# Column sums for a norm: folding 128 partitions to 64, so that one matmul with the ones replaces two

## The chip, the cores and the metric

The kernel runs on one core of a Trainium2 chip. The metric is the device time of one execution in microseconds (us); the median of three runs is taken. TensorE (PE in the rows, PEld for its weight loads), VectorE (DVE), ScalarE (ACT), GpSimd (POOL) and SyncE (SP, which only issues transfers here) run side by side and wait for one another by semaphores.

## The reference

One decoder block over 512 tokens of width 1024, all in float32:

```
h  = rms_norm(x);  [glu | q | k | v | g | gates] = h @ w_in
a  = silu(layer_norm(depthwise_conv31(glu_a * sigmoid(glu_b))));  y_a = a @ w_conv_proj + b
r  = head_norm(retention(rotary(q), rotary(k), v)) * silu(g);     y_b = r @ w_ret_proj
x  = x + (sigmoid(gA) * y_a + sigmoid(gB) * y_b) @ w_out
h2 = rms_norm(x);  x = x + (silu(u1) * u2) @ w_down   with [u1 | u2] = depthwise_conv3(h2 @ w_up)
out = rms_norm(x)
```

Each norm needs, for every token, a sum over the channels: `mean(x*x)` over 1024 channels, mean and variance over 1024 channels after the convolution, and a variance over 512 channels for each of the four retention heads.

## The kernel before

Activations lie with the channels on the 128 partitions and the 512 tokens along the free dimension, so a tensor of 1024 channels is eight tiles of 128x512. Weights arrive in pieces of 128x1024 (`wraw`), SP issuing their loads ahead of use. To keep float32 precision, each operand is cut into a rounded high part and the rest: ScalarE makes `whi` by a cast (L131), VectorE makes `wlo = wraw - whi` (L132), and every product is three matmuls (high by high, L180; high by low, L181; low by high, L182). One "unit" is 8 weight blocks times 3 matmuls, 24 matmuls into one PSUM bank. Activations are cut in the same way (`split`, L206).

A sum over channels has to cross partitions. The squares are first added tile by tile on VectorE into one tile `ss` of 128x512 (`SumSq`, L389; the adds have line L222). `sums(ss)` (L267) then cuts `ss` into `h` (ScalarE, L271) and `l = ss - h` (VectorE, L272), and later a function `run` multiplies both by a 128x128 matrix of ones, in two matmuls into one bank (L277). The result holds the channel sum of each token on all partitions. `pick` (L288) reads it into a 128x4 column, GpSimd takes the power -1/2 (L246), and two transfers carry the row out and back, spread over all partitions (`rB` or `nB`), for VectorE to multiply with.

`sums` is called eight times. In order of time, and by these numbers below:

- place 1: the first RMS norm, whose `rB` scales everything that leaves the input projection (`cosr`, L413; L417)
- places 2, 3, 4, 5: the variance of retention heads 0 to 3
- places 6, 7: mean and variance of the layer norm behind the convolution
- place 8: the RMS norm ahead of the feed-forward part

`sums` cuts at once; the matmuls come a set number of units later (`later`, `tick`), so that the engines have time for the cut in between. The convolution of 31 taps is a chain of VectorE operations (L447) with low priority, which fills VectorE wherever nothing else is due. The order on each engine is set by a scheduler when the program is built, from priorities and its own estimates of durations; on the chip each engine then takes its instructions in that written order.

Of the kernel before, what the change touches and what calls it, by code (L numbers as in the profile page):

```python
# [10 lines left out]
F32R = mybir.dt.float32r  # L11
AF = mybir.ActivationFunctionType
ALU = mybir.AluOpType

P = 128
# [34 lines left out]
def hybrid_block(  # L50
# [10 lines left out]
    nc = tc.nc  # L61
# [5 lines left out]
    def nm(s):  # L67
        uid[0] += 1
        return f"{s}_{uid[0]}"
# [3 lines left out]
    def t512(tag, bufs, dt=F32):  # L73
        if tag in first:
            t = first.pop(tag)
            assert t.dtype == dt, tag
            return t
        return sb.tile([P, S], dt, tag=tag, bufs=bufs, name=nm(tag))

    def tmp():  # L80
        return t512("t", 8)

    def bank():
        return psp.tile([P, S], F32, tag="ps", name=nm("ps"))

    def f32(ap):
        return ap.bitcast(F32)
# [19 lines left out]
    onesr = sb.tile([P, P], F32R, tag="onesr", name="onesr")  # L107
# [68 lines left out]
    def unit(ps, rhs):  # L176
        last = len(rhs) - 1
        for kt, (xh, xl) in enumerate(rhs):
            wh, wl = blocks(1)
            nc.tensor.matmul(ps, lhsT=wh, rhs=xh, start=kt == 0, stop=False)  # L180
            nc.tensor.matmul(ps, lhsT=wh, rhs=xl, start=False, stop=False)  # L181
            nc.tensor.matmul(ps, lhsT=wl, rhs=xh, start=False, stop=kt == last)  # L182
        tick()
        return ps
# [81 lines left out]

    def sums(ss):  # L267

        h = t512("t", 8, F32R)
        l = t512("t", 8, F32R)  # L270
        nc.scalar.copy(out=h, in_=ss)  # L271
        nc.vector.tensor_tensor(out=l, in0=ss, in1=f32(h), op=ALU.subtract)  # L272

        def run():
            ps = bank()
            for i, x in enumerate((h, l)):
                nc.tensor.matmul(ps, lhsT=onesr, rhs=x, start=i == 0, stop=i == 1)  # L277
            return ps

        return run  # L280
# [15 lines left out]
    def stat(ss, n, eps, use, wait, dst):  # L296

        run = sums(ss)

        def second():  # L300
            ps = run()
            r = rsqrt_eps(pick(ps, n), eps)
            row = dram.tile([P, NCH], F32, tag="row", bufs=2, name=nm("row"))
            nc.gpsimd.dma_start(out=row, in_=r)
            b = t512(dst, 1)
            flat = row.rearrange("p c -> (p c)").rearrange("(o t) -> o t", o=1)
            nc.gpsimd.dma_start(out=b, in_=flat.broadcast_to([P, S]))
            later(wait[1], lambda: use(b, ps))

        later(wait[0], second)  # L310
# [90 lines left out]
    ss = SumSq()  # L401
# [13 lines left out]
    def times_r(ps):  # L415
        t = tmp()
        nc.vector.tensor_tensor(out=t, in0=ps, in1=rB[0], op=ALU.mult)  # L417
        return t
# [6 lines left out]
    def glu_units():  # L425
        return times_r(unit(bank(), xg)), times_r(unit(bank(), xg))

    def glu_first():
        ps = unit_quad(xg)
        q1 = unit(bank(), xg)  # L430
        ts = [times_r(p) for p in ps]
        return (ts[:2], ts[2:]), q1
# [25 lines left out]
    def conv_norm():  # L458
        run = sums(csum[0])

        def centre():
            muB = t512("nB", 1)
            nc.scalar.mul(out=muB, in_=run(), mul=1.0 / D)
            sq = SumSq()
            for i in range(KT):
                nc.vector.tensor_tensor(out=accs[i], in0=accs[i], in1=muB, op=ALU.subtract)
                sq.add(accs[i])
            stat(sq.acc, D, EPS, scale, (4, 3), "nB")

        def scale(rs, _):  # L470
            for i in range(KT):
                nc.vector.tensor_tensor(out=accs[i], in0=accs[i], in1=rs, op=ALU.mult)
                t = tmp()
                nc.scalar.activation(out=t, in_=accs[i], func=AF.Silu,
                                     scale=pcol("conv_ln_g", i), bias=pcol("conv_ln_b", i))
                h = t512("A", 16, F32R)
                l = t512("C", 8, F32R)
                nc.scalar.copy(out=h, in_=t)
                nc.vector.tensor_tensor(out=l, in0=t, in1=f32(h), op=ALU.subtract)
                cv.append((h, l))  # L480

        later(4, centre)
# [115 lines left out]
    for h in range(H):  # L598
        ps, q1 = ([glu_units() for _ in range(2)], None) if h else glu_first()
# [13 lines left out]
        for e in range(DV // P):  # L613
            t = times_r(unit(bank(), xg))
# [13 lines left out]
    for mp in range(KT // 2):  # L628
        sB = [gate(KT + 2 * mp + i, tmp()) for i in range(2)]
        for i in range(2):  # L630
            m = 2 * mp + i
            ps = unit(bank(), rg)
# [3 lines left out]
    for m in range(KT):  # L636
        ps = unit(bank(), cv)
        t = tmp()
# [4 lines left out]
    ss = SumSq()  # L643
    x1 = []
    x1g = []
    for m in range(KT):
        x_ = t512("x", 8)
        nc.sync.dma_start(out=x_, in_=xT[m * P:(m + 1) * P, :])
        ps = unit(bank(), mix)
# [46 lines left out]
    ss = SumSq()  # L696
# [174 lines left out]
```

## Time and profile before

| | |
|---|---|
| median of three runs | 1071.06 us (1070.3 to 1071.65) |
| the profiled execution | 1071.72 us, of which the span of instructions is 1069.9 us |
| busy share: PE, PEld, DVE, ACT, POOL | 99%, 83%, 72%, 39%, 2% |
| granted TensorE clock, mean | 0.996 of full speed |
| matmuls in the trace | 4834, of them 16 on the line of the sums (L277) |

Times in the rows are counted from the start of the span. A row of the timeline gives start, duration, engine, line, operation, and in brackets how long the engine was idle before it and what ended that. A TensorE matmul appears as a weight load (PEld) and the matmul proper (PE); recorded durations of matmuls overlap, so their pace is read from start to start. A matmul's wait for its operands stands at its weight load.

### The profile page before, as it was taken

The numbers are of one execution on the slowest core, as the hardware profiler recorded it, in microseconds if no ns is written. First come the engines' busy times: TensorE is split into PE (matmuls) and PEld (weight loads), VectorE is DVE, ScalarE is ACT, GpSimd is POOL, SyncE is SP. The second block draws the span as 40 slices with busy tenths as digits, with TensorE's granted clock in tenths as the row PEclk, the third lists the DMA queues.
The fourth block names the chain that finished last, engine by engine and source line by source line (L and its number), as shares of the span: only waits on it lengthen the run. The fifth ranks groups of instructions, "written<-read, shape, count | busy, mean of one in ns | idle before, by whom it ended". The sixth has DMA issues, their size and how long they took to land.

```text
span 1069.9 us, 12449 instructions
## 1 busy us (share of the span) xinstructions
PE 1060.9 (99%) x4834; PEld 885.9 (83%) x4834; DVE 770.3 (72%) x1133; ACT 419.6 (39%) x561; POOL 24.4 (2%) x88
## 2 busy tenths in 40 slices
PE   9999999999999999999999999999999999999996
PEld 7888888888888888888888888888888888888886
DVE  7799899858997699957765555677776336777443
ACT  6344333533234331544552334454443113444331
POOL 0000000000000000000000000000000000000000
PEclk9999999999999999999999999999999999999998
DMA  8222232313323222223332432332222232222212
GB/s 289 91 93 102 69 99 99 108 61 103 104 89 99 70 99 99 81 78 90 108 119 97 143 119 96 106 100 99 99 99 99 99 98 93 90 96 97 99 59 79
DMA packets 34123, 107.33 MB, mean 100 GB/s; under 512 B 4048, under 2 KB 6992, under 8 KB 34064
## 3 DMA queue, kind: packets, MB, share of 16 engines
q1 hardware_dynamic: 32848, 104.42, 29.0%
q0 software_dynamic: 784, 1.85, 1.2%
q8 instruction: 38, 0.62, 0.2%
q10 hardware_dynamic: 432, 0.27, 0.1%
q14 instruction: 21, 0.17, 0.1%
HBM read 104.41 MB, written 2.11 MB: 100 GB/s over the span
## 4 chain that ended last, share of the span: by engine, by line
PE 98%; issue 1%; DVE 0%; POOL 0%; POOLq 0%; DVEq 0%
PE ps L181 27%; PE ps L180 27%; PE ps L182 27%; PE ps L507 3%; PE ps L505 3%; PE ps L506 3%; PE ps L197 2%; PE ps L563 1%; PE ps L564 1%; PE ps L562 1%; PE ps L539 0%; PE ps L541 0%; PE ps L537 0%; PE ps L318 0%; PE ps L277 0%
## 5 line engine op out<-in xcount | busy, mean ns | idle before, releaser
L131 ACT CAST whi<-wraw 128x1024 fp32r<-128x1024 f32 (+2 forms) x184 | 191.4, 1040 | 318.4 <-PE ps L181 208.3
L132 DVE TENSOR_TENSOR wlo<-wraw,whi 128x1024 fp32r<-128x1024 f32 (+2 forms) x185 | 222.6, 1203 | 59.2 <-ACT whi L131 58.0
L180 PE MATMUL ps<-xg,whi 128*128 128x512 f32 x656 | 255.6, 390 | 0.0
L181 PE MATMUL ps<-xg,whi 128*128 128x512 f32 x656 | 255.2, 389 | 0.0
L182 PE MATMUL ps<-xg,wlo 128*128 128x512 f32 x656 | 255.2, 389 | 0.0
L180 PE MATMUL ps<-A,whi 128*128 128x512 f32 x448 | 174.3, 389 | 0.0
L182 PE MATMUL ps<-A,wlo 128*128 128x512 f32 x448 | 174.3, 389 | 0.0
L447 DVE SCALAR_TENSOR_TENSOR C<-ap,par,C 128x512 f32<-128x512 f32 x240 | 166.5, 744 | 2.8 <-ACT C L444 2.6
L181 PE MATMUL ps<-A,whi 128*128 128x512 f32 x384 | 149.4, 389 | 0.0
L182 PEld LDWEIGHTS ps<-xg,wlo 128*128 128x128 f32 x656 | 123.1, 188 | 25.5
L180 PEld LDWEIGHTS ps<-xg,whi 128*128 128x128 f32 x656 | 123.2, 188 | 25.4
L181 PEld LDWEIGHTS ps<-xg,whi 128*128 128x128 f32 x656 | 123.2, 188 | 25.2
L180 PEld LDWEIGHTS ps<-A,whi 128*128 128x128 f32 x448 | 84.1, 188 | 17.6
L182 PEld LDWEIGHTS ps<-A,wlo 128*128 128x128 f32 x448 | 84.1, 188 | 17.3
L181 PEld LDWEIGHTS ps<-A,whi 128*128 128x128 f32 x384 | 72.1, 188 | 14.9
L668 DVE SCALAR_TENSOR_TENSOR t<-ap,par,t 128x512 f32<-128x512 f32 x96 | 71.7, 749 | 2.3 <-ACT t L665 0.7
L222 DVE TENSOR_TENSOR x<-x,ps 128x512 f32<-128x512 f32 (+1 forms) x50 | 32.9, 662 | 52.3 <-PE ps L182 48.8
L417 DVE TENSOR_TENSOR t<-ps,rB 128x512 f32<-128x512 f32 x48 | 32.5, 687 | 49.1 <-PE ps L182 49.1
L662 DVE TENSOR_TENSOR ap<-ps,rB 128x512 f32<-128x512 f32 x48 | 32.9, 687 | 43.5 <-PE ps L182 40.4
L180 PE MATMUL ps<-R,whi 128*128 128x512 f32 x160 | 62.2, 389 | 0.0
L181 PE MATMUL ps<-R,whi 128*128 128x512 f32 x160 | 62.2, 389 | 0.0
L182 PE MATMUL ps<-R,wlo 128*128 128x512 f32 x160 | 62.2, 389 | 0.0
(150 smaller groups left out, 1206.0 us busy)
## 6 DMA issues: line engine op xcount, KB each, us to landing
wraw<-in_wst_dram SPq DMA_DIRECT2D x180, 512.0 KB, 3.3
x<-in_xT_dram SPq DMA_DIRECT2D x16, 256.0 KB, 2.8
out_dram<-t SPq DMA_DIRECT2D x8, 256.0 KB, 2.6
nB<-row POOLq DMA_DIRECT2D x5, 256.0 KB, 4.5
dec<-in_decay_dram SPq DMA_DIRECT2D x4, 256.0 KB, 2.6
wraw<-in_wst_dram SPq DMA_DIRECT2D x3, 256.0 KB, 5.0
G<-in_wst_dram SPq DMA_DIRECT2D x2, 256.0 KB, 5.3
t<-in_cs_dram SPq DMA_DIRECT2D x2, 256.0 KB, 4.1
```

The lines of the kernel that those rows point to most:

```text
L131: (eng or nc.scalar.copy)(out=hi[:, sl], in_=raw[:, sl])
L132: nc.vector.tensor_tensor(out=lo[:, sl], in0=raw[:, sl], in1=f32(hi[:, sl]), op=ALU.subtract)
L180: nc.tensor.matmul(ps, lhsT=wh, rhs=xh, start=kt == 0, stop=False)
L181: nc.tensor.matmul(ps, lhsT=wh, rhs=xl, start=False, stop=False)
L182: nc.tensor.matmul(ps, lhsT=wl, rhs=xh, start=False, stop=kt == last)
L222: nc.vector.tensor_tensor(out=acc, in0=acc, in1=v, op=ALU.add)
L417: nc.vector.tensor_tensor(out=t, in0=ps, in1=rB[0], op=ALU.mult)
L447: nc.vector.scalar_tensor_tensor(out=acc, in0=a[:, k:k + S], scalar=wcol(k), in1=acc, op0=ALU.mult, op1=ALU.add)
L505: nc.tensor.matmul(banks[c], lhsT=xh[:, sl], rhs=wh, start=kt == 0, stop=False)
L506: nc.tensor.matmul(banks[c], lhsT=xl[:, sl], rhs=wh, start=False, stop=False)
L662: nc.vector.tensor_tensor(out=u[:, FK - 1:], in0=ps, in1=rB[0], op=ALU.mult)
L668: nc.vector.scalar_tensor_tensor(out=c, in0=u[:, k:k + S], scalar=wcol(k), in1=c, op0=ALU.mult, op1=ALU.add)
```

## The change

`sums` no longer cuts all 128 partitions. ScalarE copies partitions 64 to 127 of `ss` onto partitions 0 to 63 of a temporary `f` (L275 of the changed kernel); VectorE adds partitions 0 to 63 of `ss` to it (L276), so `f` holds 64 partial sums for each token; ScalarE rounds them into partitions 0 to 63 of `x` (L277); VectorE writes the rest, `f - x`, into partitions 64 to 127 of `x` (L278). One matmul with the ones then adds high and low parts together (L282). Two operations become four, each needing the one before; two matmuls become one.

```diff
 def sums(ss):
-    h = t512("t", 8, F32R)
-    l = t512("t", 8, F32R)
-    nc.scalar.copy(out=h, in_=ss)
-    nc.vector.tensor_tensor(out=l, in0=ss, in1=f32(h), op=ALU.subtract)
+    f = tmp()
+    x = t512("t", 8, F32R)
+    up, down = slice(0, P // 2), slice(P // 2, P)
+    nc.scalar.copy(out=f[up], in_=ss[down])
+    nc.vector.tensor_tensor(out=f[up], in0=ss[up], in1=f[up], op=ALU.add)
+    nc.scalar.copy(out=x[up], in_=f[up])
+    nc.vector.tensor_tensor(out=x[down], in0=f[up], in1=f32(x[up]), op=ALU.subtract)
     def run():
         ps = bank()
-        for i, x in enumerate((h, l)):
-            nc.tensor.matmul(ps, lhsT=onesr, rhs=x, start=i == 0, stop=i == 1)
+        nc.tensor.matmul(ps, lhsT=onesr, rhs=x, start=True, stop=True)
         return ps
     return run
```

From L283 of the changed kernel on, line numbers are 5 higher than before (L288 becomes L293, L417 becomes L422, L447 becomes L452). The scheduler also places instructions anew. On TensorE all other matmuls keep their order, and the sum's matmul keeps its place among them everywhere but at place 1.

TensorE at place 1, before (`xg` are the cut activations, `ps_313` the bank of the sums):

```order
L197 MATMUL ps_227<-xg_182,R_117 128x512
L197 MATMUL ps_228<-xg_182,R_121 128x512
L277 MATMUL ps_313<-t_221,onesr 128x512
L277 MATMUL ps_313<-t_222,onesr 128x512
L197 MATMUL ps_225<-xg_188,whi_122 128x512
L197 MATMUL ps_226<-xg_188,whi_122 128x512
```

and with the change:

```order
L197 MATMUL ps_229<-xg_182,R_117 128x512
L197 MATMUL ps_230<-xg_182,R_121 128x512
L197 MATMUL ps_227<-xg_188,whi_122 128x512
L197 MATMUL ps_228<-xg_188,whi_122 128x512
L197 MATMUL ps_229<-xg_188,R_116 128x512
L197 MATMUL ps_230<-xg_188,R_120 128x512
L197 MATMUL ps_227<-xg_189,whi_122 128x512
L197 MATMUL ps_228<-xg_189,whi_122 128x512
L197 MATMUL ps_229<-xg_189,R_116 128x512
L197 MATMUL ps_230<-xg_189,R_120 128x512
L282 MATMUL ps_315<-t_222,onesr 128x512
L197 MATMUL ps_227<-xg_188,wlo_123 128x512
```

The sum's matmul stands eight matmuls later than its two predecessors did.

VectorE at place 2, before (`ss_1012` is the head's sum of squares, `t_1028` the low part, `C_454` a convolution accumulator):

```order
L447 SCALAR_TENSOR_TENSOR C_454<-ap_451,par,C_454 128x512
L222 TENSOR_TENSOR ss_1012<-ss_1012,t_1023 128x512
L447 SCALAR_TENSOR_TENSOR C_454<-ap_451,par,C_454 128x512
L272 TENSOR_TENSOR t_1028<-ss_1012,t_1027 128x512
L417 TENSOR_TENSOR t_1062<-ps_1031,rB_78 128x512
L132 TENSOR_TENSOR wlo_1068<-wraw_1065,whi_1067 128x1024
```

and with the change (`ss_1013`, `t_1028` for `f`, `t_1029` for `x`):

```order
L452 SCALAR_TENSOR_TENSOR C_455<-ap_452,par,C_455 128x512
L222 TENSOR_TENSOR ss_1013<-ss_1013,t_1024 128x512
L132 TENSOR_TENSOR wlo_1071<-wraw_1068,whi_1070 128x1024
L276 TENSOR_TENSOR t_1028<-ss_1013,t_1028 64x512
L222 TENSOR_TENSOR ss_449<-ss_449,C_455 128x512
L422 TENSOR_TENSOR t_1065<-ps_1034,rB_78 128x512
L278 TENSOR_TENSOR t_1029<-t_1028,t_1029 64x512
```

The last convolution step and a `wlo` now come ahead of the first VectorE step of the sum, and two more operations stand between its two steps.

VectorE at place 8, before (`A_5405` is the low part of the last activation tile):

```order
L217 SCALAR_TENSOR_TENSOR A_5405<-x_5370,par,A_5404 128x512
L222 TENSOR_TENSOR ss_5122<-ss_5122,t_5408 128x512
L272 TENSOR_TENSOR t_5412<-ss_5122,t_5411 128x512
L288 SCALAR_TENSOR_TENSOR junk_5450,tok_5449<-ps_5446,ident 128x128
L288 SCALAR_TENSOR_TENSOR junk_5452,tok_5449<-ps_5446,ident 128x128
```

and with the change:

```order
L217 SCALAR_TENSOR_TENSOR A_5412<-x_5377,par,A_5411 128x512
L222 TENSOR_TENSOR ss_5129<-ss_5129,t_5415 128x512
L276 TENSOR_TENSOR t_5418<-ss_5129,t_5418 64x512
L278 TENSOR_TENSOR t_5419<-t_5418,t_5419 64x512
L132 TENSOR_TENSOR wlo_5477<-wraw_5474,whi_5476 128x1024
```

The two steps of the sum follow one another, with nothing else between them.

## Rows read from the trace of the kernel before

**Rows 1.** The page: busy time, and the chain that ended last, by engine.
```profile
PE 1060.9 (99%) x4834; PEld 885.9 (83%) x4834; DVE 770.3 (72%) x1133; ACT 419.6 (39%) x561; POOL 24.4 (2%) x88
...
PE 98%; issue 1%; DVE 0%; POOL 0%; POOLq 0%; DVEq 0%
```
**Rows 2.** Waits of the weight loads: total us, times, longest.
```profile
PEld ps L277 <- DVE t L272: 0.5, 2, 0.3
```
**Rows 3.** Line L277: min/median/max ns; then the chain: start us, us, what.
```profile
L277 PE MATMUL ps<-t,onesr x16: 388/389/499, 22.8 to 670.8; 128*128 128x512 f32 x16
...
23.00 0.59 PE ps L277 x2
23.59 5.46 PE ps L197 x24
...
116.70 0.51 PE ps L277 x2
```
**Rows 4.** Timeline around place 1, and where `rB` lands.
```profile
22.35 0.68 DVE L272 TENSOR_TENSOR t<-ss,t 128x512 fp32r<-128x512 f32 x1
...
22.61 0.19 PEld L277 LDWEIGHTS ps<-t,onesr 128*128 128x128 f32 x1
...
22.95 1.22 DVE L132 TENSOR_TENSOR wlo<-wraw,whi 128x1024 fp32r<-128x1024 f32 x1
23.09 0.19 PEld L277 LDWEIGHTS ps<-t,onesr 128*128 128x128 f32 x1 [0.29 <-DVE t L272]
...
24.09 0.28 DVE L288 SCALAR_TENSOR_TENSOR junk<-ps,ident 128x128 f32<-128x128 f32 x1
...
34.67 0.69 DVE L413 TENSOR_TENSOR cosr<-t,rB 128x512 f32<-128x512 f32 x1 [4.45 <-DMA rB<-row]
```
**Rows 5.** The stretch from place 1's `rB` to place 2: length, busy us by engine, clock.
```profile
35.30:116.00 80.70, 80.70 (x379) 68.06 (x378) 80.63 (x125) 30.77 (x47) 0.12 (x1) 1.00 0.24 82
```
**Rows 6.** Timeline around place 2.
```profile
113.92 0.76 DVE L447 SCALAR_TENSOR_TENSOR C<-ap,par,C 128x512 f32<-128x512 f32 x1
114.58 0.70 DVE L222 TENSOR_TENSOR ss<-ss,t 128x512 f32<-128x512 f32 x1
115.18 0.76 DVE L447 SCALAR_TENSOR_TENSOR C<-ap,par,C 128x512 f32<-128x512 f32 x1
115.31 0.63 ACT L271 CAST t<-ss 128x512 fp32r<-128x512 f32 x1 [8.92 <-DVE ss L222]
...
115.97 0.69 DVE L272 TENSOR_TENSOR t<-ss,t 128x512 fp32r<-128x512 f32 x1
...
116.32 0.19 PEld L277 LDWEIGHTS ps<-t,onesr 128*128 128x128 f32 x1
...
116.72 0.19 PEld L277 LDWEIGHTS ps<-t,onesr 128*128 128x128 f32 x1 [0.21 <-DVE t L272]
```
**Rows 7.** Timeline at place 7: the cut and the loads of its matmuls.
```profile
507.10 0.69 DVE L272 TENSOR_TENSOR t<-ss,t 128x512 fp32r<-128x512 f32 x1
...
512.16 0.41 PEld L277 LDWEIGHTS ps<-t,onesr 128*128 128x128 f32 x2
```
**Rows 8.** Timeline at place 8.
```profile
668.07 0.68 DVE L222 TENSOR_TENSOR ss<-ss,t 128x512 f32<-128x512 f32 x1
668.78 0.62 ACT L271 CAST t<-ss 128x512 fp32r<-128x512 f32 x1 [1.41 <-DVE ss L222]
...
670.38 0.41 PEld L277 LDWEIGHTS ps<-t,onesr 128*128 128x128 f32 x2
```
**Rows 9.** Stretches at the end: length, busy us of PE, PEld, DVE, ACT, POOL, clock.
```profile
1060.20:1061.10 0.90, 0.00 (x0) 0.00 (x0) 0.42 (x1) 0.42 (x1) 0.00 (x0) 1.00 0.16 52
1061.10:1061.80 0.70, 0.60 (x4) 0.52 (x4) 0.04 (x1) 0.51 (x1) 0.00 (x0) 1.00 1.09 379
1061.80:1062.00 0.20, 0.00 (x0) 0.00 (x0) 0.12 (x1) 0.00 (x0) 0.00 (x0) 0.76 1.10 389
1062.00:1064.00 2.00, 1.04 (x4) 0.93 (x4) 0.33 (x2) 0.00 (x0) 0.70 (x1) 0.50 0.24 82
```

## The prediction

> **What bounds the kernel now.** I read the page first: TensorE is busy for 99% of the span, and 98% of the chain that ended last runs on it [rows 1]. So time is gained by taking matmuls away and lost by making TensorE wait. The waits of its weight loads come second: on the line of the sums there are only two in the whole kernel, 0.5 us together, both for VectorE's part of the cut [rows 2]. They lie at places 1 and 2 [rows 4, 6]. Third, the pace: recorded matmuls last 0.39 us but overlap; 24 of them take 5.46 us, so one costs 0.23 us, and a pair of sums without a wait 0.45. The pair took 0.59 at place 1 and 0.51 at place 2 [rows 3], which puts 0.14 + 0.06 = 0.20 us on their waits. Last, the stretch ahead of place 2: between the landing of `rB` and place 2 VectorE is busy for 80.63 of 80.70 us [rows 5]. It has no slack there: whatever makes it start later or adds work arrives at place 2 in full.
>
> **What goes.** Eight matmuls of 0.23 us, 1.8 us in all, on the path.
>
> **What comes.** A chain of four operations, ScalarE, VectorE, ScalarE, VectorE, in place of two. No row has 64 partitions. Time goes with the elements of a partition: L288 with 128 of them takes 0.28 us, L272 with 512 takes 0.68 [rows 4]. The new operations have 512, so I take the 128x512 rows whole: 0.62 on ScalarE, 0.69 on VectorE, which starts its next 0.60 after the last [rows 6, 8]. The other end, half the lanes in half the time, would save some 0.7 us at place 2 and 1.2 at place 8. Handovers are 0.03 us between the two engines (115.31 + 0.63 to 115.97) and 0.06 from VectorE to the weight load (115.97 + 0.69 to 116.72) [rows 6]. The Trainium skill (ScalarE: Activation LUTs, section What ACT_TABLE_LOAD costs) prices an activation with constant scale and bias by the elements of a lane alone; its figures give an estimate of 0.61 us for 512, and by it the sum stays as it is; no run here shows 64 lanes.
>
> *Place 1.* The add takes the slot of the old subtract, 22.35 to 23.03. The cast then ends at 23.69, but VectorE is in a `wlo` from 22.95, so the subtract starts where the `pick` started before, at 24.09, ends at 24.77, and the load can go at 24.83 [rows 4]. The matmul's place has moved eight matmuls back, from 22.61 to 22.61 + 8 x 0.23 = 24.43. TensorE waits 0.40. Against the 0.59 of before that is 0.23 + 0.40 - 0.59 = +0.04 us. But `pick` must now wait for this matmul: 24.83 + 0.19 (load) + 0.39 (matmul) and a handover make 25.5 in place of 24.09, 1.4 us later. Power, two transfers and `cosr` hang on it, and VectorE was idle for 4.45 us ahead of `cosr`, waiting for just this [rows 4]. So its full stretch starts 1.4 us later.
>
> *Place 2.* The third add into `ss` started at 114.58. It is now later by 1.4, and by 0.66 for the convolution step that has come ahead of it (113.92 to 114.58): 116.64, ending at 117.34. Copy on ScalarE: 117.37 to 118.00, hidden by the `wlo` that VectorE takes first, from 117.24, 1.14 us (22.95 to 24.09 at place 1). Add: 118.38 to 119.07. Cast: 119.10 to 119.73, hidden by the two VectorE operations written in between, 2 x 0.60 from 118.98. Subtract: 120.18 to 120.87. Load: 120.93. TensorE arrives at 116.32 + 0.04 = 116.36 [rows 6], so it stands for 4.57 us. Everything behind it in its queue, the units of the next head, stands too. Against before: 4.57 + 0.23 - 0.51 = +4.29 us.
>
> *Places 3 to 7.* The chain has time. The tightest is place 7, where the old cut ended at 507.79 and the load came at 512.16 [rows 7]; even if the last add into `ss` (0.70) and four steps of 0.66 each came only from the old start, 507.10, they would be done at 510.4. Here only the gain counts: 5 x 0.23 = -1.15 us.
>
> *Place 8.* `ss` is complete at 668.75, and nothing stands between the steps: copy 668.78 to 669.40, add to 670.12, cast to 670.77, subtract to 671.49, load 671.55. TensorE arrives at 670.38 [rows 8]: a wait of 1.17, less one matmul, +0.94 us. The `pick` that follows moves with TensorE, so nothing further is late.
>
> Waits and matmuls together: 0.04 + 4.29 - 1.15 + 0.94 = **+4.1 us**.
>
> *The clock.* TensorE ran at full clock all through this stretch [rows 5]. At the end of the kernel TensorE is idle from 1060.2 to 1061.1, works for 0.60 us on thin matmuls of one column, and between 1061.8 and 1062.0 its granted clock falls to half, 1.2 GHz [rows 9]. The gap at place 2 is longer than that, so I expect the fall there too. At half clock a matmul of 512 columns would cost another 0.23 us. No row shows how soon the clock comes back. The ends are no matmul, if it holds, and half a unit, 12 matmuls or 2.8 us; I take seven, **1.6 us**, above the middle because this gap is all idle while the one at the end was only partly so. The Trainium skill (TensorE: Matmul & The Clock Gate, section Why this matters for your kernels) warns against idle gaps between bursts of matmuls because they put the clock back; the trace agrees at its end. By that rule the time is 1076.8, and with the clock held it would be 1075.2.
>
> **The sum.** The profiled execution took 1071.72 us, 0.66 over the median of 1071.06. 4.1 + 1.6 = 5.7 us on 1071.72 would be a profiled 1077.4; on the median it is **1076.8 us**.
>
> **The rivals.**
> 1. *The clock holds.* Same waits, no fall: 1071.06 + 4.1 = 1075.2. For it: the fall at the end came behind two gaps, with thin matmuls between. Against: each of them was shorter than this one.
> 2. *The lateness of `rB` is not passed on*, because a transfer and not `pick` decides when it lands, or because VectorE's new order saves the 1.4 us. Then place 2 waits 3.2 and the time is 1073.8 with the clock held. Against: the 4.45 us of idle and the stretch without slack [rows 4, 5].
> 3. *The other side: TensorE does not stand.* If at place 2 it took the ready matmuls behind the waiting sum, the chain would cost nothing as long as it could pass 20 of them (4.57 / 0.23). Left over would be the gain and the old waits: 1071.06 - 1.8 - 0.2 = 1069.0, not slower. Against: at place 1 the next L197 matmul was ready and still started only behind the pair, which took 0.59 in place of 0.45 [rows 3, 4].
> 4. *More is late behind place 2.* `pick`, `nB` and the head's gated values come later, and some unit waits for them or for a bank: above 1078.8. Against: from place 3 on the cuts are ready long ahead, so VectorE has slack again [rows 7].
>
> That the matmuls don't go is excluded: the written order has one for each sum.
>
> **How the numbers follow.** My forecast gets 0.48, rival 1 0.22, rival 2 0.10, rival 3 0.12, rival 4 0.08. The range is 1073.6 to 1078.8: its lower end lies under rival 2 and near rival 1 with the two places at their cheaper end (1075.2 - 1.9 = 1073.3), its upper end is the sum with the dear end of the clock (1078.0) and 0.8 for handovers that the new steps might add. Rivals 3 and 4 lie outside. A measurement of this kernel can tell about 0.2% from no change, 2.1 us. All but rival 3 are slower by more: 0.88. Rival 3 lies 0.19% below before; I count a quarter of it as faster, 0.03, the rest, 0.09, as the same.
>
> **What would show it.** Right: waits of the sum's loads for VectorE of some 0.4, 4.6 and 1.2 us at places 1, 2 and 8, none at the others; `cosr` at about 36.1; a granted clock below 1 in the microseconds behind 118. Wrong: a wait under 3 us at place 2, VectorE idle between `cosr` and place 2, 64-partition rows much shorter than 0.6 us, or a wait at places 3 to 7.

## The result, and the profile after

| | before | changed |
|---|---|---|
| median | 1071.12 us (6 runs, 1070.30 to 1071.65) | 1077.91 us (6 runs, 1075.76 to 1079.38) |
| the profiled execution | 1071.72 us, span 1069.9 | 1077.14 us, span 1075.4 |
| ratio of the times | | 1.0061, 95% interval 1.0050 to 1.0071 |

The change made the kernel 6.8 us slower; 1076.8 was forecast, from 1073.6 to 1078.8. One run, of the kernel with the later position and no fold (below), took 1795.3 us at a mean granted clock of 0.556 and is left out of that kernel's figures. The page of the changed kernel, its busy shares and the head of its chain:

```profile
PE 1060.3 (99%) x4826; PEld 884.7 (82%) x4826; DVE 776.4 (72%) x1141; ACT 425.8 (40%) x569; POOL 25.7 (2%) x88
PE 93%; DVE 5%; issue 1%; DMA 0%; ACT 0%; SPq 0%; POOLq 0%; POOL 0%; DVEq 0%
```

Against [rows 1], TensorE has eight matmuls fewer, and its share of the chain fell from 98% to 93%. VectorE has 5% of it now: the chain passes through its work ahead of place 2. What TensorE's weight loads waited for (total us, times, longest us), answering to [rows 2]; the input stage's wait for ScalarE (L197) is shown because it differs from one execution to the next, from none listed to 1.7 us in these traces:

```profile
PEld ps L282 <- DVE t L278: 5.7, 2, 4.5
PEld ps L197 <- ACT R L131: 1.4, 1, 1.4
PEld ps L282 <- issue: 0.5, 1, 0.5
```

The matmuls of the sums as one group, in place of the sixteen of [rows 3] (count, busy us, mean ns, idle time ahead of them):

```profile
L282 PE MATMUL ps<-t,onesr 128*128 128x512 f32 x8 | 3.5, 436 | 5.0 <-DVE t L278 4.9
```

**Place 1**, timeline of the changed kernel (start, us, engine, line, operation), answering to [rows 4]:

```profile
22.41 0.68 DVE L276 TENSOR_TENSOR t<-ss,t 64x512 f32<-64x512 f32 x1
24.38 0.68 DVE L278 TENSOR_TENSOR t<-t,t 64x512 fp32r<-64x512 f32 x1
25.18 0.19 PEld L282 LDWEIGHTS ps<-t,onesr 128*128 128x128 f32 x1 [0.48 <-issue]
25.71 0.29 DVE L293 SCALAR_TENSOR_TENSOR junk<-ps,ident 128x128 f32<-128x128 f32 x1 [0.65 <-PE ps L282]
36.14 0.69 DVE L418 TENSOR_TENSOR cosr<-t,rB 128x512 f32<-128x512 f32 x1 [4.29 <-DMA rB<-row]
```

The load waited 0.48 us. The view names no releaser ("issue"), but the subtract had ended only 0.12 us before it (24.38 + 0.68 = 25.06). `pick` (L293) came at 25.71 in place of 24.09, and `cosr` at 36.14 in place of 34.67: 1.47 us later.

**Place 2**, VectorE's and TensorE's timelines of the changed kernel, answering to [rows 6]:

```profile
116.04 0.77 DVE L452 SCALAR_TENSOR_TENSOR C<-ap,par,C 128x512 f32<-128x512 f32 x1
116.70 0.71 DVE L222 TENSOR_TENSOR ss<-ss,t 128x512 f32<-128x512 f32 x1
117.31 1.25 DVE L132 TENSOR_TENSOR wlo<-wraw,whi 128x1024 fp32r<-128x1024 f32 x1
118.44 0.67 DVE L276 TENSOR_TENSOR t<-ss,t 64x512 f32<-64x512 f32 x1
119.04 0.67 DVE L222 TENSOR_TENSOR ss<-ss,C 128x512 f32<-128x512 f32 x1
119.65 0.67 DVE L422 TENSOR_TENSOR t<-ps,rB 128x512 f32<-128x512 f32 x1
120.35 0.69 DVE L278 TENSOR_TENSOR t<-t,t 64x512 fp32r<-64x512 f32 x1
...
116.39 0.19 PEld L182 LDWEIGHTS ps<-xg,wlo 128*128 128x128 f32 x1
121.09 0.19 PEld L282 LDWEIGHTS ps<-t,onesr 128*128 128x128 f32 x1 [4.51 <-DVE t L278]
```

The third add into `ss` starts at 116.70, 2.1 us later than before. VectorE then works with hardly a gap until the subtract ends at 121.04, and TensorE stands for 4.51 us. Not all of this is the fold's own chain: at place 8, where nothing stands between them, the four steps take 2.71 us (673.68 to 676.39, below), and here 3.63 from the third add's end at 117.41 to 121.04. The other 0.9 us come from the `wlo` and the two operations that the scheduler put between the steps; an order without them was not tried. The same stretch by windows (us from the start of the span; length, busy us and counts of PE, PEld, DVE, ACT, POOL; granted clock; DMA share; GB/s):

```profile
120.00:121.00 1.00, 0.00 (x0) 0.00 (x0) 0.97 (x2) 0.71 (x1) 0.00 (x0) 1.00 0.81 307
121.00:122.00 1.00, 0.91 (x3) 0.74 (x4) 0.97 (x5) 0.17 (x1) 0.00 (x0) 0.68 0.34 135
122.00:123.00 1.00, 1.00 (x4) 0.81 (x3) 1.00 (x1) 1.00 (x1) 0.00 (x0) 0.50 0.00 0
123.00:124.00 1.00, 1.00 (x3) 0.73 (x3) 0.93 (x8) 0.75 (x2) 0.00 (x0) 0.50 0.00 0
124.00:125.00 1.00, 1.00 (x4) 0.82 (x3) 0.70 (x4) 0.35 (x1) 0.22 (x1) 0.61 0.72 217
125.00:126.00 1.00, 1.00 (x6) 0.78 (x5) 0.50 (x1) 0.47 (x1) 0.81 (x1) 1.00 0.79 303
```

The granted clock is full while TensorE is idle, falls to half (1.2 GHz) soon after it takes up matmuls again, and is full again before 125. The counts in a window are the matmuls under way in it; the pace is read from start to start in TensorE's timeline, here 0.43 us in place of 0.23:

```profile
122.31 0.63 PE L182 MATMUL ps<-xg,wlo 128*128 128x512 f32 x1
122.74 0.63 PE L180 MATMUL ps<-xg,whi 128*128 128x512 f32 x1
```

**Place 8**, timeline of the changed kernel, answering to [rows 8]:

```profile
673.68 0.62 ACT L275 COPY t<-ss 64x512 f32<-64x512 f32 x1 [1.41 <-DVE ss L222]
674.33 0.68 DVE L276 TENSOR_TENSOR t<-ss,t 64x512 f32<-64x512 f32 x1 [0.69 <-ACT t L275]
675.05 0.62 ACT L277 CAST t<-t 64x512 fp32r<-64x512 f32 x1 [0.75 <-DVE t L276]
675.70 0.69 DVE L278 TENSOR_TENSOR t<-t,t 64x512 fp32r<-64x512 f32 x1 [0.69 <-ACT t L277]
676.44 0.19 PEld L282 LDWEIGHTS ps<-t,onesr 128*128 128x128 f32 x1 [1.21 <-DVE t L278]
```

Four steps one behind the other, and a wait of 1.21 us. Where the time went can be read from when the first weight load of the sums starts at each place, in the two profiled executions:

| place | 1 | 2 | 3 | 4 | 5 | 6 | 7 | 8 | end of span |
|---|---|---|---|---|---|---|---|---|---|
| before | 22.61 | 116.32 | 237.12 | 357.87 | 478.62 | 489.95 | 512.16 | 670.38 | 1069.9 |
| changed | 25.18 | 121.09 | 243.15 | 363.67 | 484.19 | 495.29 | 517.28 | 676.44 | 1075.4 |
| later by | 2.57 | 4.77 | 6.03 | 5.80 | 5.57 | 5.34 | 5.12 | 6.06 | 5.5 |

Of the 2.57 at place 1, 1.8 are the eight matmuls that the sum was moved back by, which costs nothing, 0.48 is the load's wait, and the rest is the input stage, which differs between executions. What is lost behind that lies between places 1 and 3 and ahead of place 8. From place 3 to place 7 each place gives back 0.23.

### The profile page after: what moved, and what is told of

The parts are those of the page before. It is cut to its first block, busy times and chain, and to the rows that moved or that the text cites. A ratio compares the mean times of both kernels' runs of the same rounds, so it can differ in the third digit from the quotient of the medians.

```text
span 1075.4 us, 12446 instructions
## 1 busy us (share of the span) xinstructions
PE 1060.3 (99%) x4826; PEld 884.7 (82%) x4826; DVE 776.4 (72%) x1141; ACT 425.8 (40%) x569; POOL 25.7 (2%) x88
## 4 chain that ended last, share of the span: by engine, by line
PE 93%; DVE 5%; issue 1%; DMA 0%; ACT 0%; SPq 0%; POOLq 0%; POOL 0%; DVEq 0%
PE ps L180 26%; PE ps L181 26%; PE ps L182 26%; PE ps L512 3%; PE ps L511 3%; PE ps L510 3%; PE ps L197 2%; DVE C L452 2%; DVE wlo L132 1%; PE ps L568 1%; PE ps L569 1%; PE ps L567 1%; DMA x<-in_xT_dram 0%; PE ps L546 0%; PE ps L544 0%
## 5 line engine op out<-in xcount | busy, mean ns | idle before, releaser
L452 DVE SCALAR_TENSOR_TENSOR C<-ap,par,C 128x512 f32<-128x512 f32 x240 | 167.4, 755 | 2.9 <-ACT C L449 2.6
L181 PEld LDWEIGHTS ps<-xg,whi 128*128 128x128 f32 x656 | 123.6, 188 | 25.5
L422 DVE TENSOR_TENSOR t<-ps,rB 128x512 f32<-128x512 f32 x48 | 32.8, 690 | 45.4 <-PE ps L182 45.3
```

The lines of the kernel that those rows point to most:

```text
L452: nc.vector.scalar_tensor_tensor(out=acc, in0=a[:, k:k + S], scalar=wcol(k), in1=acc, op0=ALU.mult, op1=ALU.add)
```

## The experiments

The theory: the time is lost where TensorE stands (places 1, 2, 8), the part from place 1 comes in by `rB`, and behind the gap at place 2 a fall of the clock adds to it. Rivals: the clock costs nothing of note; the lateness of place 1 doesn't reach place 2; the fold itself is of no use. In the kernels of this part, each place can be folded or cut in the old way, its matmul can come later, and unneeded matmuls can be put ahead of it:

```diff
 def sums(ss):
+    place[0] += 1
+    fill = FILL.get(place[0], 0)
+    if place[0] not in FOLD:
         ...   # the old cut
+    else:
         ...   # the fold
     def run():
         ps = bank()
+        for _ in range(fill):
+            nc.tensor.matmul(ps, lhsT=onesr, rhs=xg[0][0], start=True, stop=True)
         ...
 def stat(ss, n, eps, use, wait, dst):
     run = sums(ss)
+    wait = LATER.get(place[0], wait)
```

`wait` is a pair: how many units later the sum's matmul comes, and how many units after that the norm is used. In these kernels the matmul of the sums is L297, the old cut L279 and L280, the four steps of the fold L286 to L289, the unneeded matmuls L295. The first four runs shared one chip (the kernel before: 1071.12), the next four another (1071.41), the last three a third (1071.12).

**The gap at place 2 filled.** The result of the unneeded matmuls is overwritten by the sum.

```diff
+FOLD = (1, 2, 3, 4, 5, 6, 7, 8)
+FILL = {2: 18}
```

> The whole change, and at place 2 eighteen matmuls that nobody needs (ones by the first activation tile, into the bank of the sum, overwritten by it) ahead of the sum's matmul; VectorE's order up to the sum's last step is that of the changed kernel. 18 x 0.227 = 4.1 us lie inside the wait of 4.5 us. Theory (the fall of the clock costs about 1.6 us, the wait the rest): the load of the sum's matmul still goes at 121.1 us, with a last wait of 0.4 us, the granted clock stays at 1.00 behind it, no matmul is paced at 0.43, and the time is 1.6 us under the changed kernel's profiled 1077.1, about 1075.5, with a spread as small as that of the kernel before. Rival (the clock costs nothing, the slower matmuls only take up slack): the time stays at 1077 to 1078.

Measured: 1074.80 us (1074.29 to 1075.95), ratio 1.0032 (1.0021 to 1.0044). The subtract, the weight loads and windows at place 2:

```profile
119.93 0.69 DVE L289 TENSOR_TENSOR t<-t,t 64x512 fp32r<-64x512 f32 x1
116.89 4.04 PEld L295 LDWEIGHTS ps<-xg,onesr 128*128 128x128 f32 x18
120.97 0.19 PEld L297 LDWEIGHTS ps<-t,onesr 128*128 128x128 f32 x1
...
121.00:122.00 1.00, 1.00 (x6) 0.84 (x5) 1.00 (x2) 0.58 (x1) 0.00 (x0) 1.00 0.00 0
122.00:123.00 1.00, 1.00 (x6) 0.82 (x5) 0.47 (x1) 0.99 (x2) 0.00 (x0) 1.00 0.00 0
```

The sum's load comes at 120.97 as it did at 121.09, but behind running matmuls, and the clock stays full. The last wait of 0.4 us that was expected is not there: the subtract ended at 120.62, so here the unneeded matmuls themselves held the sum up by some 0.3 us. From here to place 3's load it is 241.50 - 120.97 = 120.53 us; in the changed kernel it was 243.15 - 121.09 = 122.06. So the half clock cost 1.53 us in the profiled execution of the changed kernel. The waits, without the clock, cost 3.7 us in the medians, of which up to 0.3 may belong to the fill.

**Place 2 one unit later.**

```diff
+FOLD = (1, 2, 3, 4, 5, 6, 7, 8)
+LATER = {2: (3, 2)}     # was (2, 2)
```

> The whole change, with the sum's matmul of place 2 one unit (24 matmuls, 5.46 us) later in TensorE's order. Theory (the loss is one wait at place 2 and its clock): the subtract ends at 121.0, the matmul's turn comes at about 121.9, so there is no wait there and no fall of the clock; what is left is place 1 (0), place 2 without its old wait (-0.3), places 3 to 7 (-1.15), place 8 (+0.9): -0.5 us, 1070.6. Rival (VectorE's lateness itself costs, through banks or weights that come late): slower than before by more than 1 us, with waits of TensorE on other lines than the sums.

Measured: 1071.54 us (1070.16 to 1072.69), ratio 1.0001 (0.9992 to 1.0010). Subtract and load at place 2, and the window behind the load:

```profile
119.88 0.69 DVE L289 TENSOR_TENSOR t<-t,t 64x512 fp32r<-64x512 f32 x1
122.25 0.19 PEld L297 LDWEIGHTS ps<-t,onesr 128*128 128x128 f32 x1
122.00:123.00 1.00, 1.00 (x6) 0.82 (x5) 0.42 (x1) 0.99 (x2) 0.00 (x0) 1.00 0.00 0
```

One number in the program takes away the long wait and the clock's fall with it, and some 6 us come back. That is 0.9 us less than expected (1070.6), but inside the interval; waits of 0.6 us at place 1 and 1.2 at place 8 remain.

**The fold at place 1 alone, and at place 2 alone.**

```diff
+FOLD = (1,)      # first kernel
+FOLD = (2,)      # second kernel
```

> The fold at place 1 alone, the other seven as before. Theory (the lateness of place 1 arrives at place 2): cosr at 36.1 as in the changed kernel; the scheduler puts the convolution step and the wlo ahead of the old cut at place 2 here too, so the third add ends at about 117.4, the low part at 119.1, the second load of the pair goes at 119.1 in place of 116.7: +2.5 us, 1073.6, more only if the clock falls. Rival (place 1 costs only what its own matmul waits, 0.4 us): no difference, 1071.1, and waits at place 2 as before.

> The fold at place 2 alone. VectorE is not late here; add and subtract have one add and one wlo between them. Theory: third add ends at 115.3 as before, add 115.97, subtract 118.3 to 119.0, load 119.06, a wait of 2.7 us in place of 0.2: +2.5 us, 1073.6, if the clock holds, 1.6 more if it falls. Rival (the whole 4.5 us come from the new chain at place 2): +4.3 or more, 1075.4.

Measured: place 1 alone 1072.96 us, ratio 1.0016 (1.0007 to 1.0025); place 2 alone 1073.11, ratio 1.0021 (1.0012 to 1.0030). VectorE's third add and low part and the two loads of the old pair at place 2 in the first kernel, then the load of the second with a window behind it:

```profile
115.76 0.68 DVE L222 TENSOR_TENSOR ss<-ss,t 128x512 f32<-128x512 f32 x1
117.50 0.68 DVE L280 TENSOR_TENSOR t<-ss,t 128x512 fp32r<-128x512 f32 x1
117.14 0.19 PEld L297 LDWEIGHTS ps<-t,onesr 128*128 128x128 f32 x1 [1.57 <-ACT t L279]
118.23 0.19 PEld L297 LDWEIGHTS ps<-t,onesr 128*128 128x128 f32 x1 [0.90 <-DVE t L280]
```
```profile
117.85 0.19 PEld L297 LDWEIGHTS ps<-t,onesr 128*128 128x128 f32 x1 [2.31 <-DVE t L289]
118.00:119.00 1.00, 1.00 (x5) 0.82 (x6) 1.00 (x2) 0.00 (x0) 0.00 (x0) 1.00 0.93 213
```

The first kernel has the old cut at place 2, and still TensorE waits 1.57 + 0.90 = 2.47 us there. Not all of that is lateness: as expected, the scheduler gave VectorE another order at place 2 here too, with a convolution step (0.66) ahead of the third add, and 1.74 us from the third add to the low part in place of 1.39 [rows 6]. These make 1.0 us, and 0.2 were there before. The other 1.3 us agree with the 1.4 that were forecast for the lateness of `pick`. So what place 1 loses is paid some 90 us later at place 2, and rival 2 falls. The two kernels' waits, 2.47 and 2.31, add up to 4.78, near the 4.51 of both folds together, though VectorE's order is another in each of the three. In neither profile did the clock fall, though TensorE stood for over 2 us.

**Places 3 to 7 alone, and place 8 alone.**

```diff
+FOLD = (3, 4, 5, 6, 7)      # first kernel
+FOLD = (8,)                 # second kernel
```

> The fold at places 3 to 7 alone, where the chain has time. Theory (a matmul taken away is worth its pace, 0.23 us): no waits on the sums beyond the two of before, -1.15 us, about 1069.95. Rival (the gain is lost in waits elsewhere, or a matmul is worth its recorded 0.39 us): 1071.1, or 1069.1.

> The fold at place 8 alone. Theory: a wait of 1.2 us for the subtract, less one matmul: +0.9 us, about 1072.0, with the granted clock at 1.00 around it. Rival (the wait takes the place of a later one, as VectorE waits for the row of rB anyway): no difference, 1071.1 or 0.2 less.

Measured: places 3 to 7, 1070.10 us, ratio 0.9991 (0.9982 to 1.0000), which is -1.3 us; place 8, 1071.98, ratio 1.0008 (0.9999 to 1.0016), +0.6 us. At places 3 to 7 no load waits. At place 8 it is the same wait as in the changed kernel:

```profile
671.03 0.19 PEld L297 LDWEIGHTS ps<-t,onesr 128*128 128x128 f32 x1 [1.21 <-DVE t L289]
```

The signs are as expected, and five matmuls less are worth five times 0.23. Each of the two effects is near what the runs can tell from nothing.

**Versions that should beat both.** First the fold where the chain has time, the old cut at places 1 and 8; then the fold at place 8 too, with its matmul a unit later.

```diff
+FOLD = (2, 3, 4, 5, 6, 7)              # first kernel
+LATER = {2: (3, 2)}
+FOLD = (2, 3, 4, 5, 6, 7, 8)           # second kernel
+LATER = {2: (3, 2), 8: (2, 2)}         # place 8 was (1, 3)
```

> The fold at places 2 to 7, old cut at 1 and 8, and the matmul of place 2 one unit later. Theory: no waits for the chain anywhere but the 0.3 us of place 1: six matmuls and the old wait of place 2 gone, -1.4 us, about 1069.7. Rival (the later sum of head 0 makes its norm late): a new wait on a line of the next head's projection, 1071 or more.

> As e7_best, and the fold at place 8 too, with its matmul one unit later and the use of rB where it was, so one unit is left for the way of rB in place of two. Theory: the chain is hidden at place 8, another -0.23 us, about 1069.5, if rB lands before the banks run out. Rival (rB comes up to 5.2 us later, VectorE starts the feed-forward part later, and the banks hold TensorE up): waits of TensorE for VectorE behind place 8, up to 5 us, 1071 to 1075.

Measured: 1070.44 us (1069.99 to 1071.02), ratio 0.9991 (0.9982 to 1.0000), and 1069.67 (1068.99 to 1070.31), ratio 0.9985 (0.9976 to 0.9993). The first gains 1.0 us where 1.4 were expected; its old pair at place 1 waited 0.7 us in place of 0.3. The second is faster than the kernel before by 1.7 us and than the changed kernel by some 8. Its place 8:

```profile
668.75 0.69 DVE L289 TENSOR_TENSOR t<-t,t 64x512 fp32r<-64x512 f32 x1 [0.69 <-ACT t L288]
673.75 0.19 PEld L297 LDWEIGHTS ps<-t,onesr 128*128 128x128 f32 x1
```

The subtract ends 4.3 us before the load is due. No load of the sums waits anywhere in this execution.

**The later position without a fold**, to see which of the two gains.

```diff
+FOLD = ()
+LATER = {2: (3, 2), 8: (2, 2)}
```

> No fold: the old cut and two matmuls at all eight places, those of places 2 and 8 one unit later. Theory (the fold's gain is the matmul left out, 7 x 0.23 = 1.6 in the best version; moving alone only saves the old wait of 0.06 at place 2): within 0.3 us of the kernel before. Rival (the later position is what gains): 1.4 to 1.8 us faster than the kernel before, like the best version.

Measured: 1071.26 us (ten runs, 1070.58 to 1072.39), ratio 1.0002 (0.9993 to 1.0012). Moving alone gains nothing; the gain of the best version agrees with its seven matmuls, 7 x 0.23 = 1.6 us.

**The changed kernel again, beside the fill, on one chip.** The first is the changed kernel as it is, the second the fill from above.

> The changed kernel once more, beside the next two. Clock theory (TensorE's clock falls behind the gap at place 2, for a stretch that differs from one execution to the next): about 1077, that is +5.7 on the kernel before, single runs spread over some 3 us. Rival (the first runs owed part of their length to their chip): below +4.6, no more above the fill than its own spread.

> The gap at place 2 filled with 18 unneeded matmuls, as in the first fill, on the same chip as the changed kernel. Clock theory: 1.6 to 2 us below the changed kernel, +4.0 on the kernel before, runs spread by less than 2 us. Rival: same time as the changed kernel, since the wait itself is kept.

Measured: changed kernel 1076.75 us (1075.80 to 1077.68), ratio 1.0053 (1.0039 to 1.0067); fill 1074.53 (1074.15 to 1075.70), ratio 1.0034 (1.0021 to 1.0046). With the gap filled 2.2 us come back, and each run of the changed kernel lies above each of the fill, so the clock theory holds. The wide scatter did not come again on this chip: 1.9 us against 1.6 of the fill. Place 1 to 2 of this second execution of the changed kernel: `pick`, `cosr`, the load at place 2, windows behind it, and the head of the chain that ended last:

```profile
24.77 0.29 DVE L293 SCALAR_TENSOR_TENSOR junk<-ps,ident 128x128 f32<-128x128 f32 x1 [0.66 <-PE ps L282]
34.53 0.69 DVE L418 TENSOR_TENSOR cosr<-t,rB 128x512 f32<-128x512 f32 x1 [3.62 <-DMA rB<-row]
119.51 0.19 PEld L282 LDWEIGHTS ps<-t,onesr 128*128 128x128 f32 x1 [3.90 <-DVE t L278]
119.00:120.00 1.00, 0.49 (x2) 0.45 (x3) 0.97 (x2) 0.13 (x1) 0.00 (x0) 1.00 0.64 258
120.00:121.00 1.00, 1.00 (x5) 0.81 (x4) 1.00 (x4) 0.75 (x1) 0.00 (x0) 0.66 0.00 0
121.00:122.00 1.00, 1.00 (x4) 0.71 (x4) 0.96 (x5) 0.99 (x2) 0.00 (x0) 0.50 0.00 0
PE 86%; DVE 9%; issue 2%; DMA 1%; ACT 1%; POOL 0%; SPq 0%; POOLq 0%; DVEq 0%
```

The wait at place 2 is 3.90 here in place of 4.51, 0.61 less. The way from `pick` to `cosr` is 34.53 - 24.77 = 9.76 us in place of 36.14 - 25.71 = 10.43, 0.67 less. So in these two executions the time from `pick` over the power and the two transfers to `cosr` decides, within 0.1 us, how long TensorE stands 85 us later. The chain that ended last shows the same path: here it leaves TensorE at place 1, goes through `pick`, the power, the row out (2.35 us) and back (4.12 us) and `cosr`, stays on VectorE for 85 us, and comes back to TensorE with the load at 119.51. The clock fell here too, and to place 3's load (241.58) it was 122.07 us, as in the first execution; in the second fill, from 120.65 to 241.10, it was 120.45.

## Why the prediction was right, step by step

- **Pace and gain.** Each place from 3 to 7 gives back 0.23 us in the table of starts, as the sum had it; no wait at these places.
- **64 partitions.** The price was the open end: half the lanes for half the time, or the whole. The new rows take 0.62 us on ScalarE and 0.67 to 0.69 on VectorE, as much as the 128x512 rows of [rows 6, 8]. So time went with the elements of a partition here, and the fold adds two full operations a place. The Trainium skill (ScalarE: Activation LUTs, section What ACT_TABLE_LOAD costs) prices by the elements of a lane; the estimate from it was 0.61, and the trace agrees with 0.62.
- **Place 1.** `pick` was forecast at 25.5 and `cosr` at 36.1; they came at 25.71 and 36.14. The load's wait was put at 0.40, and it was more, 0.48 to 0.89, in all six traces that fold place 1.
- **Place 2.** The load was forecast at 120.93 with a wait of 4.57 us; it came at 121.09 with 4.51. The terms hold too: with place 1 left as it was the wait is 2.31, and place 1 alone makes 2.47, with the scheduler's new order in it. The full VectorE is what carries the lateness so far.
- **Place 8.** Forecast a wait of 1.17, measured 1.21.
- **The clock.** 1.6 us was forecast, from seven matmuls at half pace; in the two profiled executions of the changed kernel it was 1.53 and 1.54 (122.06 and 122.07 in place of 120.53; 0.08 more against the second fill), eight matmuls or so at 0.43 us in place of 0.23. That this number came so near is in good part luck: seven was a choice between the ends none and twelve, and no row of before showed it. The Trainium skill (TensorE: Matmul & The Clock Gate, section Why this matters for your kernels) warns of idle gaps between bursts of matmuls; the trace agrees at place 2 with 0.50 behind a gap of 4.51 us. Rival 1 falls.

By these terms the profiled execution was forecast at 1077.4, and it took 1077.14. Rival 3 falls with every wait at the sums: matmuls behind the waiting one did not pass it. Of rival 4 nothing shows in the profiled executions: TensorE's list of waits has none that the kernel before lacks but those on L282.

In the medians two terms are off, in opposite directions, so it is in part luck that the sum came within 1.1 us. **The waits** were put at +4.1 us together; with the gap filled they cost 3.7 and 3.4. The step that was mis-sized is the wait at place 2, because it was worked out from one execution, in which the way from `pick` to `cosr` took 34.67 - 24.09 = 10.58 us [rows 4]. That is the longest of the 13 profiled executions of this study; the shortest has 9.72, the middle one 10.16. The fold at place 2 alone shows it: its way took 10.16 us, 0.42 less, and it waited 2.31 us where 2.7 were expected. So an execution with the middle value waits some 0.4 us less at place 2, while the kernel before, which had no more than 0.2 us of waits there to lose, gains next to nothing by it. The single folds point the same way: place 1 was expected at +2.5 us and measured at +1.8, place 2 at +2.5 and +2.0, place 8 at +0.9 and +0.6, each with the expected value inside its interval.

**The clock** was put at +1.6 us; by the medians, changed kernel less fill, it cost 3.1 and 2.2. The second figure rests on five runs each, which scatter by 1.6 to 1.9 us, so it cannot be told from the 1.5 of the profiles. The first has two parts. The first three of the six runs of the changed kernel (1075.76 to 1077.14 us, mean granted clock 0.996) have their middle 1.2 us above the fill; the last three (1078.69 to 1079.38 us, 0.993) have it 4.1 us above. At half clock, 0.003 less in the mean is 2 x 0.003 x 1076 = 6.5 us more at half pace, and that costs 3.2 us (2 to 4, as the means are rounded to 0.001); the two middles lie 2.9 us apart. So by these means TensorE was at half pace for longer in those three executions than in either that was profiled. Where, and whether the gap at place 2 was the cause, stays open: none of them has a trace, they came one after the other, and the five later runs of the changed kernel, 1075.80 to 1077.68 us, do not reach them.

## What to carry to other kernels

On VectorE and ScalarE the rows of 512 elements took as long on 64 partitions as on 128, so halving the partitions halved nothing; a fold that saves one 0.23 us matmul and lengthens the chain ahead of it by two operations pays only where the chain has time, and there it pays in full. When a step moves later, follow it through the busy engine: behind a VectorE without slack a delay of 1.4 us arrived 85 us later as a wait of TensorE. Before giving up such a change, look for the number that sets when its result is due: one unit later at two places, with the old cut kept at place 1, turned 6.8 us lost into 1.7 us gained.

## What was not expected of the hardware

- The clock did not fall in the gap but after it. Through 4.5 us without a matmul the granted clock read 1.00; it read half from some 0.3 us after matmuls came again (0.68 over 121 to 122 is 0.64 us at half), and in the second profiled execution only after TensorE had been working for some 0.8 us (0.66 over 120 to 121, behind a load at 119.51). Whoever reads the clock over the idle time alone sees nothing of it. The gaps of 2.3 us, or of 1.6 and 0.9 one after the other, left it full in their profiled executions.
- VectorE's subtract at place 2, which writes partitions 64 to 127, started at 120.35, 0.70 us after the start of the operation ahead of it and behind its end at 120.32; its neighbours follow one another at 0.60 to 0.61, before the one ahead has ended. The operation behind it, on all partitions again, started 0.71 us later (121.06). The handovers inside VectorE were forecast at 0.60 throughout. Why this one is held was not tried.
